# Encoder block on one core: opening stage reordered, factors and copies moved from VectorE to ScalarE

## The chip, the cores and the metric

The kernel runs on one core of one Trainium2 chip. The metric is the device time of one execution in microseconds (us). Engines are named as in the profile: PE (TensorE matmul), PEld (its weight loads), DVE (VectorE), ACT (ScalarE), POOL (GpSimd) and SP (SyncE, which here only issues transfers).

## The reference, cut to what matters

```
mod = silu(c) @ w_ada + b_ada;  shift, scale, gate = split(mod, 3)
h   = rms_norm(x, norm_w) * (1 + scale) + shift          # 1024 x 1024
proj = h @ w_in                                          # eight column groups
r_q, r_k, r_v, r_g, m_cq, m_ckv, m_kr, m_g = split(proj)
rq, rk = rope(r_q, positions), rope(r_k, positions) * 64**-0.5
lg_f, lg_b = log_sigmoid(decay logits)                   # one per head
scores = (q . k) * decay_mask(lg); cross = (q * exp(lg*(i+1))) . state
...                                                      # group norm, attention group, output projection, residual
```

The opening stage computes `h` transposed (the "features"), the first retention projection, and three things that depend on small inputs alone: the decays `lg` with the masks made from them, and the cosine and sine tables of the rotary embedding.

## The kernel before, in words

All matrices are 1024 wide and cut into 128-row tiles: eight feature tiles `k`, eight sequence tiles `t`. Products are made to full precision by splitting each operand into a high and a low part (`hh`/`hl` for features, `wh`/`wl` for weight pages) and adding three matmuls (lines 65 to 67).

The opening goes as follows. `x_tile(t)` squares and sums a tile of x, takes the power on POOL (L158), scales the tile on DVE (L159), transposes it on PE and copies the two halves to `xn`, half 0 by ACT (L166), half 1 by DVE (L168). `modulation(k)` makes two sums over 1024 columns on DVE (L178) and from them two factors per feature (L181, L183). `features(k, half)` applies the factors on ACT (L188), rounds to `hh` on ACT (L189) and takes the rest `hl` on DVE (L190). `products(k, lo, hi)` adds feature tile `k`'s 12 matmuls for four sequence tiles. The eight sums `acc0` occupy all eight PSUM banks until feature 7 is in.

Then each of the four head groups `g` runs: for a tile `t` of sums, ACT copies the value part `v` (L355), DVE multiplies the query and key part by the cosine table `Cr` and the sine table `Sr` (L364, L366), POOL combines (L370, L371), and so on. The first `gate` matmuls of group 0 need a PSUM bank, and that is free only when `v`, L364 and L366 of tile 0 have read it.

A weight page comes through `wpage`: a transfer of 512 KB into one of two `wr` buffers, a cast on ACT (`wh`, L80) and a subtraction (`wl`, L81) on POOL; the four pages of the opening take DVE for that. A third page's transfer must wait for the first page's subtraction.

The program is written as a data flow; a scheduler turns it into one fixed order per engine, and each engine executes its own list in that order. `tc.issue_after(ins)` holds the instructions traced inside it behind `ins` in the list of `ins`'s engine; others of the block are free. Before the change only the masks and the two Sin activations stand behind such a mark (the ACT cast of feature `KACT = 1`); decays (L236 to L260) and table arithmetic (L280 to L315) are placed wherever the scheduler saw room.

Of the kernel before, what the change touches and what calls it, by code (L numbers as in the profile page):

```python
# [12 lines left out]
AF = mybir.ActivationFunctionType  # L13
ALU = mybir.AluOpType
# [16 lines left out]
def body(tc, I, O):  # L31
    nc = tc.nc
    V, A, G, T, SY = nc.vector, nc.scalar, nc.gpsimd, nc.tensor, nc.sync
# [50 lines left out]
    def wpage(src, n, k, pool=None, tag="wr", bufs=2):  # L84
        raw = (pool or p_ring).tile([P, n], F32, name="wr", tag=tag, bufs=bufs)
        SY.dma_start(out=raw, in_=src)
        return split(raw, (("p (k n) -> p k n",), {"k": k}))
# [10 lines left out]
    hh = [p_h.tile([P, S], F32R, name=f"hh{k}", tag=f"hh{k}") for k in range(KT)]  # L98
    hl = [p_h.tile([P, S], F32R, name=f"hl{k}", tag=f"hl{k}") for k in range(KT)]
# [25 lines left out]
    xn = p_st.tile([P, KT, S], F32, name="xn", tag="xn")  # L125
# [22 lines left out]
    def x_tile(t, bank):  # L148

        x_ = ld["x", t]  # L150
        if t in XDVE:
            V.scalar_tensor_tensor(out=xn[:, :, ts_(t)], in0=x_.rearrange("p (a b) -> p a b", b=P), scalar=1.0,
                                   in1=x_.rearrange("p (a b) -> p a b", b=P), op0=ALU.mult, op1=ALU.mult,
                                   accum_out=msq[:, t:t + 1])
        else:
            A.activation(xn[:, :, ts_(t)], x_.rearrange("p (a b) -> p a b", b=P), AF.Square, accum_out=msq[:, t:t + 1])
        V.tensor_scalar(out=msq[:, t:t + 1], in0=msq[:, t:t + 1], scalar1=1.0 / D, scalar2=EPS, op0=ALU.mult, op1=ALU.add)
        G.tensor_tensor(out=r_x[:, t:t + 1], in0=msq[:, t:t + 1], in1=neghalf[:, 0:1], op=ALU.pow)  # L158
        V.tensor_scalar(out=x_, in0=x_, scalar1=r_x[:, t:t + 1], scalar2=None, op0=ALU.mult)  # L159
        for z in range(2):  # L160
            ps = bank()
            for q in range(4):
                T.transpose(ps[:, ts_(q)], x_[:, ts_(4 * z + q)], ident)
            dst, src = xn[:, 4 * z:4 * z + 4, ts_(t)], ps.rearrange("p (a b) -> p a b", a=4)
            if z == 0:
                A.copy(out=dst, in_=src)  # L166
            else:
                V.tensor_copy(out=dst, in_=src)  # L168

    b1s = {}  # L170
    c1 = ctile("c1", KT)
    V.scalar_tensor_tensor(out=c1, in0=bada[:, KT:2 * KT], scalar=1.0, in1=nw, op0=ALU.add, op1=ALU.mult)

    def modulation(k):
        mp = p_st.tile([P, 2], F32, name="mp", tag="mp", bufs=3)
        for i, kind in enumerate("sb"):
            wa = ld[kind, k]
            V.scalar_tensor_tensor(out=wa, in0=wa, scalar=1.0, in1=sc, op0=ALU.mult, op1=ALU.mult,  # L178
                                   accum_out=mp[:, i:i + 1])
        b1 = p_st.tile([P, 2], F32, name="b1", tag="b1", bufs=3)  # L180
        V.scalar_tensor_tensor(out=b1[:, 0:1], in0=mp[:, 0:1], scalar=nw[:, k:k + 1], in1=c1[:, k:k + 1],  # L181
                               op0=ALU.mult, op1=ALU.add)
        V.tensor_tensor(out=b1[:, 1:2], in0=mp[:, 1:2], in1=bada[:, k:k + 1], op=ALU.add)  # L183
        b1s[k] = b1

    def features(k, half):
        sl = slice(half * 512, half * 512 + 512)
        A.activation(xn[:, k, sl], xn[:, k, sl], AF.Identity, bias=b1s[k][:, 1:2], scale=b1s[k][:, 0:1])  # L188
        i0 = A.copy(out=hh[k][:, sl], in_=xn[:, k, sl])  # L189
        V.tensor_tensor(out=hl[k][:, sl], in0=xn[:, k, sl], in1=hh[k][:, sl], op=ALU.subtract)  # L190
        return i0

    w0, acc0 = [], []

# [22 lines left out]
    for k in range(KT):  # L217
        if k:
            modulation(k)
        if k % 2 == 0 and k + 2 < KT:  # L220
            load(("w", k // 2 + 1))
        if 3 <= k + 2 < KT:
            load(("s", k + 2), ("b", k + 2))
        if k and k % 2 == 0:
            w_page(k // 2)
        for half in range(2):
            if k or half:
                i0 = features(k, half)
                products(k, 4 * half, 4 * half + 4)
            if k == KACT:  # L230
                x_last = i0


    lg = ctile("lg", 16)
# [29 lines left out]
    after = ExitStack()  # L264
    after.enter_context(tc.issue_after(x_last.ins))
    for h in range(H):
# [17 lines left out]
                    in1=posf.unsqueeze(2).broadcast_to([P, NT, 32]), op=ALU.mult)  # L284
# [26 lines left out]
    after = tc.issue_after(x_last.ins)  # L311
# [4 lines left out]
    A.activation(Cr, nn, AF.Sin)  # L316
    after.__exit__(None, None, None)

    st.close()


# [14 lines left out]
            pending.pop(0)()  # L336

    for g in range(4):
        w = w0 if g == 0 else [wpage(I["w_ret"][g][j], 1024, 2) for j in range(4)]
        vv = []  # L340
        ST = p_ret.tile([P, NT, 2, P], F32, name="ST", tag="ST")
        sT = [None] * NT
        qdT = [None] * NT
        for t in range(NT):
# [13 lines left out]
            if g == 0 and NACC <= t < NB0:  # L358
# [6 lines left out]
                            in1=Cr[:, t:t + 1].broadcast_to([P, 8, 32]), op=ALU.mult)  # L365
# [23 lines left out]
            for h in range(2):  # L389
# [3 lines left out]
                            op=ALU.mult)  # L393
# [19 lines left out]
                                       op0=ALU.mult, op1=ALU.add)  # L413


        wg = [wpage(I["w_rg"][g][j], 1024, 4) for j in range(2)]
        sg = p_ret.tile([P, 2, S], F32, name="sg", tag="sg")
        def gate(h):
            for half in range(2):
# [494 lines left out]
PREP_0 = (2, 4, 5, 6, 6)  # L914
NB0, NACC, XW = 8, 4, 8
WLX = (6, 7)
XDVE, KACT = (3, 6), 1
MG0 = 2
PEND = 1
EARLY = (2, 6)  # L920
# [70 lines left out]
```

## Time and profile before

| | us |
|---|---|
| median of 3 timed runs (1050.13 to 1053.33) | 1051.39 |
| the profiled execution | 1050.91 |
| its span | 1048.8 |
| PE busy in the span | 1014.0 |
| DVE busy in the span | 565.3 |
| first gate matmul of group 0 starts at | 82.74 |

A span counts from the first to the last instruction; 2.1 us of the execution lie outside it. "Busy" is time in which an engine had an instruction in work. A row of a timeline gives the start, the duration (of all, where x2 or more are merged), the engine, the source line and the operation, then output<-inputs; in brackets the engine's idle time just before and what ended it. Instructions of one engine overlap a little at their ends, so that the next starts some 0.07 us before the end shown.

### The profile page before, as it was taken

The numbers are of one execution on the slowest core, as the hardware profiler recorded it, in microseconds if no ns is written. First come the engines' busy times: TensorE is split into PE (matmuls) and PEld (weight loads), VectorE is DVE, ScalarE is ACT, GpSimd is POOL, SyncE is SP. The second block draws the span as 40 slices with busy tenths as digits, with TensorE's granted clock in tenths as the row PEclk, the third lists the DMA queues.
The fourth block names the chain that finished last, engine by engine and source line by source line (L and its number), as shares of the span: only waits on it lengthen the run. The fifth ranks groups of instructions, "written<-read, shape, count | busy, mean of one in ns | idle before, by whom it ended". The sixth has DMA issues, their size and how long they took to land.

```text
span 1048.8 us, 15165 instructions
## 1 busy us (share of the span) xinstructions
PE 1014.0 (97%) x5704; PEld 885.8 (84%) x5704; DVE 565.3 (54%) x1294; ACT 430.2 (41%) x864; POOL 406.5 (39%) x311
## 2 busy tenths in 40 slices
PE   5899999999999999999999999989999999989998
PEld 4687888888888888998888889879999999878887
DVE  7995447445355433046202116777877787882342
ACT  6654313313312312134322016567777777772100
POOL 2233315313411421125634127943466554873210
PEclk8899999999999999999999999999999999999999
DMA  9721103102101203233744420100000000003522
GB/s 369 263 63 58 41 1 121 41 2 80 61 21 41 66 27 114 82 121 101 236 160 170 157 86 1 41 1 2 21 22 21 2 21 22 21 21 121 172 99 71
DMA packets 30744, 82.27 MB, mean 78 GB/s; under 512 B 3536, under 2 KB 4560, under 8 KB 30672
## 3 DMA queue, kind: packets, MB, share of 16 engines
q1 hardware_dynamic: 25920, 72.92, 20.4%
q10 hardware_dynamic: 4752, 8.39, 2.2%
q8 instruction: 45, 0.74, 0.3%
q14 instruction: 27, 0.22, 0.1%
HBM read 64.52 MB, written 16.78 MB: 78 GB/s over the span
## 4 chain that ended last, share of the span: by engine, by line
PE 48%; DVE 4%; ACT 1%; DMA 1%; issue 1%; POOL 1%; ACTq 0%; DVEq 0%; POOLq 0%
PE pt L763 5%; PE acc L65 4%; PE acc L66 4%; PE sp L65 4%; PE acc L67 4%; PE sp L67 4%; PE sp L66 4%; PE po L66 3%; PE po L67 3%; PE po L65 3%; PE sm L66 1%; PE sm L65 1%; PE sm L67 1%; PE pt L676 1%; PE pt L65 1%; PE pt L67 1%
## 5 line engine op out<-in xcount | busy, mean ns | idle before, releaser
L81 POOL TENSOR_TENSOR wl<-wr,wh 128x1024 fp32r<-128x1024 f32 (+2 forms) x51 | 116.2, 2288 | 172.5 <-ACT wh L80 153.8
L65 PE MATMUL acc<-wh,hh 128*128 128x512 f32 (+2 forms) x352 | 131.1, 372 | 1.7 <-ACT hh L189 1.7
L66 PE MATMUL acc<-wl,hh 128*128 128x512 f32 (+2 forms) x352 | 130.8, 372 | 0.0
L67 PE MATMUL acc<-wh,hl 128*128 128x512 f32 (+2 forms) x352 | 126.6, 368 | 2.1 <-DVE hl L190 2.1
L749 POOL TENSOR_SCALAR pr<-pr,st 128x1024 f32<-128x1024 f32 x62 | 72.1, 1166 | 101.2 <-DVE st L748 77.9
L65 PE MATMUL acc<-hh,wh 128*128 128x512 f32 x256 | 101.1, 395 | 1.8 <-ACT v L355 1.8
L766 DVE TENSOR_TENSOR pl<-pt,ph 128x512 fp32r<-128x512 f32 x128 | 85.7, 683 | 31.2 <-ACT ph L765 31.2
L66 PE MATMUL acc<-hl,wh 128*128 128x512 f32 x256 | 101.0, 394 | 0.0
L67 PE MATMUL acc<-hh,wl 128*128 128x512 f32 x256 | 100.6, 393 | 0.0
L80 ACT CAST wh<-wr 128x1024 fp32r<-128x1024 f32 (+2 forms) x55 | 53.7, 982 | 104.8 <-PE sm L66 45.3
L765 ACT CAST ph<-pt 128x512 fp32r<-128x512 f32 x128 | 73.2, 590 | 27.9 <-PE pt L763 25.8
L747 ACT ACTIVATE pr<-sp,st 128x1024 f32<-128x1024 f32 x62 | 69.5, 1121 | 22.9 <-DVE st L745 22.7
L370 POOL TENSOR_TENSOR rb<-t,t 128x128 f32<-128x128 f32 x32 | 16.1, 502 | 160.4 <-PE sm L379 61.2
L66 PE MATMUL po<-pl,vh 128*128 128x256 f32 x256 | 76.4, 298 | 1.9 <-DVE pl L766 1.9
L744 DVE TENSOR_REDUCE st<-sp 128x1 f32<-128x1024 f32 x62 | 75.4, 1216 | 4.6 <-PE sp L67 4.5
L65 PEld LDWEIGHTS acc<-wh,hh 128*128 128x128 f32 x352 | 67.2, 191 | 10.6 <-ACT hh L189 2.1
L67 PEld LDWEIGHTS acc<-wh,hl 128*128 128x128 f32 x352 | 66.0, 188 | 10.8 <-DVE hl L190 3.0
L66 PEld LDWEIGHTS acc<-wl,hh 128*128 128x128 f32 x352 | 67.3, 191 | 8.6
L65 PE MATMUL po<-ph,vh 128*128 128x256 f32 x256 | 73.7, 288 | 0.0
L763 PE MATMUL pt<-ident,pr 128*128 128x128 f32 x496 | 70.2, 274 | 3.0 <-DVE st L748 2.7
L67 PE MATMUL po<-ph,vl 128*128 128x256 f32 x256 | 72.8, 285 | 0.0
L763 PEld LDWEIGHTS pt<-ident,pr 128*128 128x128 f32 x496 | 58.1, 141 | 7.5 <-issue 2.9
(354 smaller groups left out, 2463.4 us busy)
## 6 DMA issues: line engine op xcount, KB each, us to landing
x<-w_ada SPq DMA_DIRECT2D x16, 512.0 KB, 7.0
wr<-w_ret SPq DMA_DIRECT2D x16, 512.0 KB, 3.5
wr<-w_rg SPq DMA_DIRECT2D x8, 512.0 KB, 3.5
retD<-ro SPq DMA_DIRECT2D x16, 256.0 KB, 2.0
wr<-w_mg SPq DMA_DIRECT2D x8, 512.0 KB, 3.5
wa<-w_ada SPq DMA_DIRECT2D x8, 512.0 KB, 3.7
wr<-w_out SPq DMA_DIRECT2D x8, 512.0 KB, 4.5
wro<-retD SPq DMA_DIRECT2D x8, 512.0 KB, 3.9
```

The costliest lines, as they stand in the source:

```text
L65: T.matmul(out, lh, rh, start=first, stop=False, **kw)
L66: T.matmul(out, lh, rl, start=False, stop=False, **kw)
L67: return T.matmul(out, ll, rh, start=False, stop=last, **kw)
L80: A.copy(out=hi, in_=raw)
L81: eng.tensor_tensor(out=lo, in0=raw, in1=hi, op=ALU.subtract)
L370: G.tensor_tensor(out=rv[:, :, 0], in0=t1[:, :, 0], in1=t2[:, :, 1], op=ALU.subtract)
L744: V.tensor_reduce(out=st_[:, 0:1], in_=sp, op=ALU.max, axis=AX.X)
L747: A.activation(pr, sp, AF.Exp, bias=st_[:, 1:2], scale=sc_, accum_out=st_[:, 2:3])
L749: G.tensor_scalar(out=pr, in0=pr, scalar1=st_[:, 3:4], scalar2=0.0, op0=ALU.mult, op1=ALU.add)
L763: T.transpose(tp[:, ts_(q)], pr[:, ts_(half * 4 + q)], ident)
L765: A.copy(out=ph[half][:, :, c_], in_=tv)
L766: V.tensor_tensor(out=pl[half][:, :, c_], in0=tv, in1=ph[half][:, :, c_], op=ALU.subtract)
```

## The change

Four parts. (1) The copies of half 1 of tiles 0 to 3 go from DVE to ACT, and so does the square of tile 3 (`XDVE`). (2) The two factors per feature tile are made by ACT activations on [128 x 1] operands and no longer by DVE. (3) Every DVE instruction of the decays, masks and tables stands behind the `hl` subtraction of feature 5 (`KACT = 5`, `late`), and their marked ACT instructions behind its cast. (4) The ACT casts of the next weight pages (two gate pages of group 0, four pages of group 1) stand behind the last feature cast `f_last`. The transfers are on SP's list and carry no mark; the POOL subtractions follow their casts.

```
-            if z == 0:
+            if z == 0 or t < 4:
                 A.copy(out=dst, in_=src)
...
-        V.scalar_tensor_tensor(out=b1[:, 0:1], in0=mp[:, 0:1], scalar=nw[:, k:k + 1], in1=c1[:, k:k + 1],
-                               op0=ALU.mult, op1=ALU.add)
-        V.tensor_tensor(out=b1[:, 1:2], in0=mp[:, 1:2], in1=bada[:, k:k + 1], op=ALU.add)
+        A.activation(b1[:, 0:1], mp[:, 0:1], AF.Identity, bias=c1[:, k:k + 1], scale=nw[:, k:k + 1])
+        A.activation(b1[:, 1:2], mp[:, 1:2], AF.Identity, bias=bada[:, k:k + 1])
...
             if k == KACT:
-                x_last = i0
+                x_last, v_last = i0
+
+    f_last = i0[0]
+    late = ExitStack()
+    late.enter_context(tc.issue_after(v_last.ins))
...
+    late.close()
     st.close()
...
     for g in range(4):
+        after = ExitStack()
+        if g < 2:
+            after.enter_context(tc.issue_after(f_last.ins))
         w = w0 if g == 0 else [wpage(I["w_ret"][g][j], 1024, 2) for j in range(4)]
+        after.close()
...
+        after = ExitStack()
+        if g == 0:
+            after.enter_context(tc.issue_after(f_last.ins))
         wg = [wpage(I["w_rg"][g][j], 1024, 4) for j in range(2)]
+        after.close()
...
-XDVE, KACT = (3, 6), 1
+XDVE, KACT = (6,), 5
```

What became of the order shows at the hand-over from the last feature to the first gate matmul. ACT's list before, from the last feature casts (`hh_91`) to the copies of `v`:

```order
L189 CAST hh_91<-xn 128x512 x2
L272 ACTIVATE mask<-mt 128x128 x2
L80 CAST wh<-wr 128x1024
L313 ACT_TABLE_LOAD
L313 ACTIVATE Sr<-rtmp 128x256
L316 ACTIVATE Cr<-rtmp 128x256
L80 CAST wh<-wr 128x1024
L355 COPY v<-acc 128x256 x4
```

The same stretch of ACT's list in the changed program, from the instruction behind the last `hh_91` on (line numbers there are shifted by -1 to +12; left out are the three small decay activations L261, L262 and L259):

```order
L80 CAST wh<-wr 128x1024 x4
L316 ACT_TABLE_LOAD
L316 ACTIVATE Sr<-rtmp 128x256
L319 ACTIVATE Cr<-rtmp 128x256
L261 ACT_TABLE_LOAD
...
L270 ACTIVATE qfac<-small,lgs 128x128 x8
L275 ACTIVATE mask<-mt 128x128
L80 CAST wh<-wr 128x1024
L275 ACTIVATE mask<-mt 128x128 x2
L80 CAST wh<-wr 128x1024
L275 ACTIVATE mask<-mt 128x128 x5
L363 COPY v<-acc 128x256 x4
```

Between the last feature cast and the first copy of `v` there are now six page casts, two table loads, and all of `qfac` and `mask`; a third table load, for the decays' first Exp, stands just ahead of the last `hh_91`.

DVE's list before, ahead of the first product with `Cr` (L364), where the masks were long made:

```order
L291 SCALAR_TENSOR_TENSOR rtmp<-rtmp 128x256 x2
L310 TENSOR_SCALAR rtmp<-rtmp 128x256
L314 SCALAR_TENSOR_TENSOR rtmp<-rtmp 128x256
L315 TENSOR_SCALAR rtmp<-rtmp 128x256
L364 TENSOR_TENSOR t_759<-acc,Cr 128x256
L366 TENSOR_TENSOR t_760<-acc,Sr 128x256
```

and in the changed program (`rtmp` is the tables' scratch, `m_` and `mt` the masks' exponents; L372 and L374 are the old L364 and L366):

```order
L318 TENSOR_SCALAR rtmp<-rtmp 128x256
...
L252 SCALAR_TENSOR_TENSOR lg<-lt_628,lt_629 128x16
...
L273 TENSOR_SCALAR m_669<-small,lg 128x128
L274 SCALAR_TENSOR_TENSOR mt<-small,lg,m_669 128x128
...
L273 TENSOR_SCALAR m_711<-small,lg 128x128
L274 SCALAR_TENSOR_TENSOR mt<-small,lg,m_711 128x128
L277 TENSOR_SCALAR mask<-mask 128x1024
L372 TENSOR_TENSOR t_759<-acc,Cr 128x256
L374 TENSOR_TENSOR t_760<-acc,Sr 128x256
```

Eight pairs of mask exponents and the scaling of the whole mask, which waits for the last mask activation, now stand between the end of the tables and the first product with `Cr`.

## Rows read from the trace of the kernel before

**Rows 1.** Busy time by stretch; columns: length, five engines, PE clock, DMA share, GB/s

```profile
0.00:10.00 10.00, 4.72 (x21) 4.46 (x22) 4.38 (x28) 7.15 (x12) 1.83 (x8) 1.00 0.81 301
10.00:20.00 10.00, 5.51 (x29) 4.72 (x27) 9.64 (x27) 5.41 (x10) 2.56 (x3) 0.84 1.03 413
60.00:250.00 190.00, 187.57 (x986) 158.94 (x985) 106.54 (x303) 59.20 (x146) 58.74 (x61) 1.00 0.14 45
```

**Rows 2.** Timeline of PE: products of the opening, then the first gate matmul

```profile
34.01 0.80 PE L65 MATMUL sm<-wh,hh 128*128 128x512 f32 x1 [2.60 <-ACT hh L189]
...
51.13 0.63 PE L65 MATMUL acc<-wh,hh 128*128 128x512 f32 x1
51.56 0.63 PE L66 MATMUL acc<-wl,hh 128*128 128x512 f32 x1
...
80.29 0.39 PE L66 MATMUL sm<-wl,hh 128*128 128x512 f32 x1
80.52 0.39 PE L67 MATMUL sm<-wh,hl 128*128 128x512 f32 x1
82.74 0.47 PE L65 MATMUL acc<-hh,wh 128*128 128x512 f32 x1 [1.84 <-ACT v L355]
```

**Rows 3.** Timeline of POOL: subtractions of weight pages

```profile
46.25 5.92 POOL L81 TENSOR_TENSOR wl<-wr,wh 128x1024 fp32r<-128x1024 f32 x2 [18.61 <-ACT wh L80]
62.57 5.84 POOL L81 TENSOR_TENSOR wl<-wr,wh 128x1024 fp32r<-128x1024 f32 x2 [10.40 <-DVE mt L271]
...
74.39 2.64 POOL L81 TENSOR_TENSOR wl<-wr,wh 128x1024 fp32r<-128x1024 f32 x1
```

**Rows 4.** Timeline of DVE: instructions that ran beside those, and L364

```profile
47.02 2.31 DVE L181 SCALAR_TENSOR_TENSOR b<-mp,small,c 128x1 f32<-128x1 f32 x1
...
49.85 3.40 DVE L178 SCALAR_TENSOR_TENSOR x<-x,sc 128x1024 f32<-128x1024 f32 x1
...
74.71 2.60 DVE L291 SCALAR_TENSOR_TENSOR rtmp<-rtmp 128x256 f32<-128x256 f32 x1
...
81.84 0.42 DVE L364 TENSOR_TENSOR t<-acc,Cr 128x256 f32<-128x256 f32 x1 [1.83 <-ACT v L355]
```

**Rows 5.** Timeline of DVE: the same kinds of instruction undisturbed

```profile
22.66 0.34 DVE L271 SCALAR_TENSOR_TENSOR mt<-small,lg,m 128x128 f32<-128x128 f32 x1
...
27.78 0.74 DVE L159 TENSOR_SCALAR xl<-xl,r_x 128x1024 f32<-128x1024 f32 x1
28.45 1.21 DVE L178 SCALAR_TENSOR_TENSOR x<-x,sc 128x1024 f32<-128x1024 f32 x1
...
29.59 0.68 DVE L168 COPY xn<-sm 128x512 f32<-128x512 f32 x1
30.19 0.20 DVE L181 SCALAR_TENSOR_TENSOR b<-mp,small,c 128x1 f32<-128x1 f32 x1
...
38.30 0.68 DVE L190 TENSOR_TENSOR hl<-xn,hh 128x512 fp32r<-128x512 f32 x1
...
73.88 0.91 DVE L274 TENSOR_SCALAR mask<-mask 128x1024 f32<-128x1024 f32 x1
...
78.00 0.88 DVE L291 SCALAR_TENSOR_TENSOR rtmp<-rtmp 128x256 f32<-128x256 f32 x2
```

**Rows 6.** Timeline of ACT

```profile
38.26 1.85 ACT L267 ACTIVATE qfac<-small,lgs 128x128 f32<-128x128 f32 x6
...
61.45 1.04 ACT L80 CAST wh<-wr 128x1024 fp32r<-128x1024 f32 x1
...
64.59 1.52 ACT L188 ACTIVATE xn<-xn,b 128x512 f32<-128x512 f32 x2
...
69.81 1.12 ACT L189 CAST hh<-xn 128x512 fp32r<-128x512 f32 x2
...
74.33 1.28 ACT L313 ACT_TABLE_LOAD   x1
```

**Rows 7.** Transfers issued in the first 100 us: KB each, median us to landing

```profile
wr<-w_ret SPq DMA_DIRECT2D x9, 512.0 KB, 3.5
```

More of the change, by code (lines that the diff above doesn't have):

```diff
@@ L189, in features @@
         i0 = A.copy(out=hh[k][:, sl], in_=xn[:, k, sl])
-        V.tensor_tensor(out=hl[k][:, sl], in0=xn[:, k, sl], in1=hh[k][:, sl], op=ALU.subtract)
-        return i0
+        i1 = V.tensor_tensor(out=hl[k][:, sl], in0=xn[:, k, sl], in1=hh[k][:, sl], op=ALU.subtract)
+        return i0, i1
     w0, acc0 = [], []
```

## Prediction

> **What bounds the kernel now.** I read the busy time by stretch first. After 60 us PE is the bound and hardly waits: busy 187.57 of 190 us in the stretch to 250 [rows 1]. So whatever moves the start of that stretch moves the end of the kernel by the same amount, and the question is when PE can start its first gate matmul, at 82.74 in the profiled execution [rows 2].
>
> Next I read PE's own timeline. Its last product of the opening starts at 80.52, then it waits 1.84 us for ACT's copy of v and for what stands behind that, because all eight PSUM banks hold sums that nobody has read [rows 2]. The hand-over (tables ready, v copied, L364 and L366 done, PE starts) is the place that sets everything behind it. Before it PE is fed by DVE: in 10 to 20 us DVE is busy 9.64 of 10 us, PE 5.51 [rows 1].
>
> Third, POOL and DVE side by side. Two page subtractions on POOL run from 46.25 to 52.17 and one from 74.39 to 77.03 [rows 3]. Beside the first two, a DVE instruction on 128x1 elements takes 2.31 us and one on 128x1024 takes 3.40; beside the third, L291 takes 2.60 [rows 4]. Undisturbed the same kinds take 0.20, 1.21 and 0.46 (half of 0.88, with the step to the next) [rows 5]. So each subtraction stops DVE for 2.1 to 2.2 us. The two subtractions at 62.57 do it twice more: five of five that met such DVE work. One DVE instruction gets through between two subtractions that follow each other.
>
> **What the change gives the opening.** DVE loses four copies (0.60 each, from one start to the next), one square (1.14) and 16 factors (about 0.13 each): 5.6 us. It also loses the decays, masks and tables ahead of feature 5, and the two stops of 2.2 us at 46 to 52, since those casts now stand behind the last feature. ACT gains 4 copies, a square and 16 small activations, and has room.
>
> How early the last feature cast, T, then comes, by DVE's list: the first w_ada row cannot be in before 0.29 + 5 x 0.524 = 2.9 MB have arrived, 9.7 us at 301 GB/s; the second needs about 11 us [rows 1]. From there to the last of the 16 sums DVE has 16 x 1.14 (L178) + 5 x 0.67 (L159) + 5 x 1.14 (four page subtractions and the square of tile 6) + 4 x 0.60 (L168) + 10 x 0.60 (L190) + 0.4 of small ones = 36.1 us [rows 5]. I add 2.5 us for waits on ACT's first page cast and on POOL's powers (an estimate; 0 to 5), which gives 49.6. Then ACT: factors 0.2, two L188 1.4, a cast 0.5, the table load 1.28, an Exp 0.1, the last cast 0.5 [rows 6]: T = 53.7, where the features before ran to about 71.
>
> PE does not reap it there. Its 180 products behind 34.01 cost 0.227 us each, 41 us [rows 2]; started 2 to 4 us earlier and without stalls they end at 72 to 75 instead of 81. Then the banks are full, as before.
>
> **What the change puts on the hand-over.** Behind T, ACT's list has four page casts, Sin, Exp, qfac, masks with two more casts, and only then the copies of v. Counted from T:
>
> First the tables. The casts (0.95 each) let POOL subtract from T+1.0 to T+6.9 (2.9 each, as in the disturbed pairs [rows 3]). The third page's transfer waits for the first subtraction and lands 3.5 us after its issue [rows 7], so it is cast at T+8.4 and subtracted until T+11.1; the fourth is cast at T+11.4 and subtracted until T+14.1. DVE has 18 table instructions behind the last hl: 11 at 0.46 and 7 single-source ones at about 0.3, 7.2 us [rows 5]. Between the stops it gets 0.95, 0.6, 2.1 and 0.6 us; the other 2.9 follow T+14.0. The last one that Sr needs ends at T+16.9, Cr is complete at **T+18.1**.
>
> Then the masks, counted from Cr: an Exp load 1.28, three small Exp 0.5, eight qfac 2.35 (6 took 1.85), a mask 0.2, the fifth page's cast 0.95 [rows 6]. So the fifth and sixth subtractions run from +5.3 to +11.1 and stop DVE in the middle of the mask exponents, of which only two are buffered. The rest, a remainder of 0.3 and three pairs at 0.6, ends at +13.0; the last mask activation 0.25, the scaling of the mask 0.83 (L274), and two products with Cr and Sr 0.75: PE starts at **Cr + 14.9** [rows 4, 5].
>
> Sum: 53.7 + 18.1 + 14.9 = 86.7 against 82.74, **+4.0 us**. PE has then been idle for 12 to 14 us. In the opening, after 2.60 us of idleness, and again near 51, products start 0.43 us apart instead of 0.227, the lower of the clock's two levels (1.2 GHz) [rows 2]; that lasted for 8 and about 10 products, 1.6 and 1.9 us lost. I take +1.7 (0, as after the 1.84 us of idleness, to 3.5). Together +5.7 on the execution of 1050.91: **1056.6 us**. That execution is 0.5 below the median of the three timed runs, 1051.39, so this is +0.5% on the median.
>
> The remaining edits cost nothing of their own. The factors' ACT activations lie under DVE's sums, which ACT waits for anyway; if ACT had no room there, 32 halves of features would shift by some 0.1 us each, before T. Page transfers for group 1 are issued by SP in the same sequence, and its pages are needed only after four gate passes of 24 products, 20 us behind the hand-over.
>
> Two rules of the Trainium skill bear on this. The page "SBUF — State Buffer", section "SBUF: two separate sides", says that VectorE and GpSimd share one port pair as an exclusive lock, that a VectorE instruction with two SBUF inputs or in a two-port mode needs it, and that the loser blocks for the whole instruction. The rows show 2.1 to 2.2 of 2.6 to 2.9 us; by the rule the six stops would be some 0.3 us longer each, and the sum about 1.5 us more, 1058. "ScalarE: Activation LUTs", section "What ACT_TABLE_LOAD costs", puts a drain of about 1.38 us on top of 1.28 for each switch. The row shows 1.28; by the rule the two loads on the path (ahead of T, and behind Cr) would add 2.8 us, 1059.4.
>
> **The rivals.** (a) *The stops do not add up: faster.* If POOL's subtractions find gaps of DVE's chain, whose instructions wait for one another, or delay only work that ACT's list delays anyway, the tables are bound by the casts: two subtractions of 2.4 end at T+5.8, the fourth cast at T+10.3, Sin load, Sr and Cr at T+12.4, and the masks take 10.0 instead of 14.9. PE starts at 53.7 + 22.4 = 76.1, waits 1 to 4 us, loses 1.6 to the clock: 77.7, -5.0, 1046 us. Were the tables ready before PE, the floor is PE's own 72 to 75: 1042. Against it: five of five stops. The six stops cost the path 10.6 us in the sum (5.7 in the tables, 4.9 in the masks); the sign turns where they cost less than 4.9, and the gain can be told below 1.7.
>
> (b) *Only the tables are stopped.* The fifth and sixth casts come where DVE has the mask exponents done, or POOL gets the lock late: 53.7 + 18.1 + 10.0 = 81.8, +1.7 clock: +0.8, 1051.7, no difference that can be told. For it: the mask exponents are short, so a race of 0.3 us decides one of them.
>
> (c) *Worse:* DVE waits more in the opening (T at 57), or the later pages land 2 us later each with transfers under way: +3 to +4 on the sum, 1060.5.
>
> (d) *The opening is not relieved at all,* because transfers bound it: 28 tiles of 0.524 MB at 413 GB/s end near 38 us, ahead of the last sums at 48. T moves only if this were 10 us off; I leave it in (c).
>
> **How the numbers follow.** The sum as made: 0.57; (c) and (d): 0.06; (b): 0.15; (a): 0.22. Faster by over 0.3% (3.2 us, about what a measurement of this kernel can tell from no change) is (a), 0.22. Within it: (b) and a small part of the sum with T at 51, together 0.17. Slower 0.61. The sum's own range is 1053.5 to 1060.5 (T 2.5 us either way, the clock 0 to 3.5). The range for 8 in 10 has to reach into (a), down to 1046, where half of (a) lies, and up to 1061.5 for most of (c).
>
> **What the profile after would show.** Right, step by step: the last feature cast at 52 to 56; no DVE instruction of the features above 2 us; PE's products unbroken from some 31 us and done at 72 to 75; four subtractions on POOL within 14 us behind the last cast, each with one DVE table instruction of about 2.5 us beside it; Cr some 18 us behind the last cast; two more such pairs among the mask exponents; an idle time of PE of 10 us and more that ends with L374 or the copy of v; products 0.43 apart after it. Wrong: an idle time of PE under 5 us there, tables' instructions at 0.4 beside the subtractions, or a last feature cast before 50.

## The result: 0.6% slower

The changed kernel takes 1056.16 us (median of 6 runs, 1054.07 to 1056.76); the kernel before, run beside it, 1050.14 (6 runs, 1047.92 to 1053.33). The ratio is 1.0056, 95% interval 1.0039 to 1.0073. Forecast were 1056.6 us and slower with a chance of 0.61. The profiled execution took 1055.9 us with a span of 1053.8, so 5.0 more than the profiled one of before; by the medians the changed kernel takes 6.0 more.

I read the changed kernel's profile in the order of the prediction: busy time by stretch first, columns as in [rows 1].

```profile
10.00:20.00 10.00, 4.49 (x26) 3.67 (x27) 6.47 (x12) 8.88 (x18) 2.56 (x3) 0.71 1.03 412
20.00:30.00 10.00, 8.55 (x44) 7.17 (x42) 9.19 (x17) 6.40 (x14) 4.39 (x3) 0.78 1.03 409
...
80.00:90.00 10.00, 0.74 (x2) 0.67 (x3) 8.85 (x14) 4.41 (x15) 5.31 (x6) 0.50 0.30 105
...
60.00:250.00 190.00, 174.96 (x916) 148.13 (x914) 103.07 (x304) 57.83 (x148) 57.47 (x58) 0.96 0.15 51
```

From 60 to 250 us TensorE is now busy 174.96 us instead of 187.57 [rows 1]. The loss lies at the hand-over: in the row from 80 to 90 us TensorE is busy 0.74 us, at a granted clock of 0.50. In the two stretches of the opening VectorE has 3.5 and 0.8 us to spare; in the first of them it had 0.4 before. This comes up again below. TensorE's own timeline has the place itself (start, duration, operation, and the idle time with what ended it):

```profile
73.83 0.39 PE L67 MATMUL sm<-wh,hl 128*128 128x512 f32 x1
89.26 0.76 PE L65 MATMUL acc<-hh,wh 128*128 128x512 f32 x1 [15.04 <-DVE t L374]
89.83 0.63 PE L66 MATMUL acc<-hl,wh 128*128 128x512 f32 x1
90.25 0.63 PE L67 MATMUL acc<-hh,wl 128*128 128x512 f32 x1
```

The opening's products are done at 74.2 instead of 80.9 [rows 2], and nothing comes of it: TensorE idles 15.04 us, starts its first gate product 6.5 us later than before, and then has starts 0.42 to 0.43 us apart, the lower level of the clock. What it waited for stands on GpSimd and VectorE. First GpSimd's timeline of the changed kernel from 55 to 92 us:

```profile
57.22 4.94 POOL L81 TENSOR_TENSOR wl<-wr,wh 128x1024 fp32r<-128x1024 f32 x2 [30.64 <-ACT wh L80]
64.27 5.17 POOL L81 TENSOR_TENSOR wl<-wr,wh 128x1024 fp32r<-128x1024 f32 x2 [2.11 <-DVE lt L249]
79.32 4.69 POOL L81 TENSOR_TENSOR wl<-wr,wh 128x1024 fp32r<-128x1024 f32 x2 [9.88 <-ACT wh L80]
```

Beside these, in VectorE's timeline of the same stretch, stand six instructions over 2 us:

```profile
57.34 2.37 DVE L244 TENSOR_TENSOR lt<-lt,lt 128x16 f32<-128x16 f32 x1
...
59.83 2.36 DVE L245 TENSOR_TENSOR lt<-lt 128x16 f32<-128x16 f32 x1
...
64.49 2.37 DVE L248 TENSOR_TENSOR lt<-lt,lt 128x16 f32<-128x16 f32 x1
...
67.12 2.36 DVE L249 TENSOR_SCALAR lt<-lt 128x16 f32<-128x16 f32 x1
...
79.49 2.33 DVE L274 SCALAR_TENSOR_TENSOR mt<-small,lg,m 128x128 f32<-128x128 f32 x1 [0.47 <-ACT mask L275]
81.85 2.74 DVE L273 TENSOR_SCALAR m<-small,lg 128x128 f32<-128x128 f32 x1
```

Six page subtractions, six instructions of VectorE that take 2.33 to 2.74 us instead of the 0.17 to 0.35 that the same kinds take elsewhere in this timeline; these are the lines that answer to [rows 3, 4]. ScalarE's timeline of the changed kernel, in the same stretch, shows the chain that runs through them:

```profile
54.16 1.28 ACT L241 ACT_TABLE_LOAD   x1
...
55.58 0.61 ACT L188 CAST hh<-xn 128x512 fp32r<-128x512 f32 x1
56.10 1.99 ACT L80 CAST wh<-wr 128x1024 fp32r<-128x1024 f32 x2
...
73.45 0.42 ACT L319 ACTIVATE Cr<-rtmp 128x256 f32<-128x256 f32 x1 [0.37 <-DVE rtmp L318]
73.89 1.28 ACT L261 ACT_TABLE_LOAD   x1
75.18 0.30 ACT L261 ACTIVATE kfac<-lg,small 128x8 f32<-128x8 f32 x1
...
87.64 1.18 ACT L363 COPY v<-acc 128x256 f32<-128x256 f32 x4
```

The last feature cast ends at 56.2 (the expectations below say 56.1, which is where the next cast starts), Cr is complete at 73.87, and the copies of v start only at 87.64, behind the last mask.

### The profile page after: what moved, and what is told of

It is laid out like the page before. It is cut to its first block, busy times and chain, and to the rows that moved or that the text cites. A ratio compares the mean times of both kernels' runs of the same rounds, so it can differ in the third digit from the quotient of the medians.

```text
span 1053.8 us, 15175 instructions
## 1 busy us (share of the span) xinstructions
PE 1011.0 (96%) x5704; PEld 884.5 (84%) x5704; DVE 559.5 (53%) x1272; ACT 439.2 (42%) x887; POOL 404.7 (38%) x311
## 4 chain that ended last, share of the span: by engine, by line
PE 48%; DVE 3%; ACT 1%; DMA 1%; issue 1%; POOL 1%; ACTq 0%; DVEq 0%; POOLq 0%
PE pt L775 5%; PE acc L65 4%; PE sp L65 4%; PE acc L66 4%; PE acc L67 4%; PE sp L67 4%; PE sp L66 4%; PE po L66 3%; PE po L67 3%; PE po L65 3%; PE sm L66 1%; PE sm L65 1%; PE sm L67 1%; PE pt L688 1%; PE pt L65 1%; PE pt L66 1%
## 5 line engine op out<-in xcount | busy, mean ns | idle before, releaser
L80 ACT CAST wh<-wr 128x1024 fp32r<-128x1024 f32 (+2 forms) x55 | 53.7, 982 | 112.4 <-PE sm L66 42.3
L65 PEld LDWEIGHTS acc<-hh,wh 128*128 128x128 f32 x256 | 48.5, 189 | 25.3 <-ACT v L363 15.4
```

Source lines behind the costliest of these rows:

```text
L65: T.matmul(out, lh, rh, start=first, stop=False, **kw)
L80: A.copy(out=hi, in_=raw)
```

## The experiments

The theory that went into them: each GpSimd subtraction that runs beside tables or masks holds one VectorE instruction for its whole length, these stops add up along the chain from the last feature to the v copies, and TensorE, with all banks full, waits for that chain. The main rival (A): the order on ScalarE (casts, table loads, qfac, masks, then v) sets the hand-over, whatever GpSimd does.

**1. The stops taken away.** The edit, on the changed kernel as in all runs (here and below a long line is cut to the call that changes, and lines that only hand an argument on are left out):

```diff
+        if not low:
+            A.copy(out=hi, in_=raw)
+            v_ = hi.rearrange(*shape[0], **shape[1])
+            return v_, v_
...
-wpage(I["w_ret"][g][j], 1024, 2)
+wpage(I["w_ret"][g][j], 1024, 2, low=g != 1)
-wpage(I["w_rg"][g][j], 1024, 4)
+wpage(I["w_rg"][g][j], 1024, 4, low=g > 1)
```

> The changed kernel, with the low halves of the weight pages behind the features (w_ret of the second group, w_rg of the first two) left out: their high half stands in for it, so GpSimd has no subtraction between the features and the masks. Loads, casts, table loads and the order on ScalarE stay. My theory (six GpSimd subtractions each stop one table or mask instruction of VectorE for 2.1 to 2.5 us, and the chain from Cr to the v copies hands that on): the stopped instructions go back to 0.2 to 0.4 us, Cr complete 7 to 9 us sooner (65 to 67 instead of 73.9), the first gate product at 76 to 79 instead of 89.3, TensorE's wait before it 2 to 5 us instead of 15.0, time 1042 to 1046. Rival A (ScalarE's list decides: three table loads, four casts, eight qfac, eight masks ahead of the v copies, whatever GpSimd does): gate product at 86 or later, time 1053 to 1057. Rival B (only the stops in the tables lie on the path, those in the masks are hidden): gate product at 80 to 82, 1047 to 1050.

Measured: 1052.88 us, ratio to before 1.0022 (1.0012 to 1.0033). GpSimd has no subtraction between the features and the gate product, the tables' instructions take 0.16 to 0.43 us each and the masks' exponents 0.28 to 0.35. This kernel's timeline of TensorE has the end of the opening and the first gate product:

```profile
74.31 0.39 PE L67 MATMUL sm<-wh,hl 128*128 128x512 f32 x1
79.30 0.77 PE L65 MATMUL acc<-hh,wh 128*128 128x512 f32 x1 [4.59 <-DVE t L378]
```

The gate product comes at 79.30, 10.0 us sooner than with the stops, after 4.59 us of idleness instead of 15.04. That was the theory's number (76 to 79) within 0.3 us, and rival A's (86 or later) is off by 7. 0.9 of the 10.0 us is an earlier last feature cast (55.3). Cr is complete at 67.6, not quite at the expected 65 to 67. ScalarE's timeline of this kernel has the reason:

```profile
64.51 1.05 ACT L80 CAST wh<-wr 128x1024 fp32r<-128x1024 f32 x1 [1.21 <-DMA wr<-w_ret]
...
67.20 0.40 ACT L323 ACTIVATE Cr<-rtmp 128x256 f32<-128x256 f32 x1
```

With no subtraction to wait for, a fifth page is cast ahead of the table load, and Sr and Cr follow that load without a wait: once the stops are gone, the page casts and the transfers that they wait for set Cr. In all, seven page casts stand ahead of v here instead of six, so ScalarE has more to do there than in the changed kernel, and rival A is out all the same. Rival B (gate product at 80 to 82) is only 0.7 us off; against it stands that the gate product follows Cr by 11.7 us here and by 15.4 in the changed kernel. The total is not what I expected: 3.3 us below the changed kernel instead of 10 to 14. The lead is 9.1 us at TensorE's matmul 400, counted from 0 (106.88 against 115.96), and 8.1 at matmul 3600 (712.26 against 720.34), but 4.3 at matmul 4200 (800.25 against 804.53). It goes in the attention stage, far from the edited pages; from 720 to 780 us TensorE is busy 58.98 us there, where the changed kernel has 60.00. The next part comes back to that.

**2. The tables early again, all else kept.**

```diff
-    late.enter_context(tc.issue_after(v_last.ins))
...
-XDVE, KACT = (6,), 5
+XDVE, KACT = (6,), 1
```

> The changed kernel without its part that puts decays, masks and rotary tables behind the features; copies and factors on ScalarE stay, and so do the pages held behind the last feature. My theory (the table and mask work between features and v copies, with the stops in it, makes the hand-over late; taken into the features it fills VectorE there at its undisturbed price): last feature cast 4 to 8 us later than 56.1 (60 to 64), but Cr and the masks ready within 12 to 16 us of it, first gate product at 76 to 80, time 1043 to 1049, so faster than both. Rival (the held pages are the cost, wherever the tables stand): gate product at 86 or later, time 1053 to 1057. Rival C (VectorE's sum is what counts and nothing is gained by order): gate product at 82 to 84, time 1049 to 1052.

Measured: 1044.76 us, ratio 0.9954 (0.9938 to 0.9971): faster than before, and 11.4 us below the changed kernel. This kernel's timeline of ScalarE, with the last feature casts and the first copies of v:

```profile
54.61 1.12 ACT L188 CAST hh<-xn 128x512 fp32r<-128x512 f32 x2
...
76.79 1.19 ACT L362 COPY v<-acc 128x256 f32<-128x256 f32 x4
```

And of TensorE, its one wait from 70 to 95 us:

```profile
78.09 0.47 PE L65 MATMUL acc<-hh,wh 128*128 128x512 f32 x1 [1.59 <-ACT v L362]
```

The time and the gate product are as expected, one number is not: I had the last feature cast at 60 to 64, since VectorE now does decays, masks and part of the tables ahead of it. It ends at 55.7, as early as with the late tables (56.2). From 10 to 30 us VectorE is busy 18.4 us here against 15.7 in the changed kernel (busy time by stretch of experiment 2; columns: length, VectorE's busy time, TensorE's clock, DMA share, GB/s):

```profile
10.00:20.00 10.00, 8.87 (x27) 0.82 1.03 413
20.00:30.00 10.00, 9.56 (x17) 0.84 1.03 409
```

The early decays and masks fill time in which VectorE otherwise waits (for what, the groups under experiment 7 show). With the pages held, as here, taking them out gave the features nothing; putting them behind the features added them to the chain.

**3. The pages no longer held.**

```diff
-        if g < 2:
-            after.enter_context(tc.issue_after(f_last.ins))
...
-        if g == 0:
-            after.enter_context(tc.issue_after(f_last.ins))
```

> The changed kernel without the hold of the next weight pages behind the last feature; copies, factors and the late tables stay. My theory (the pages find a free buffer and a place on ScalarE only near the end of the features anyway, so their subtractions meet the tables with or without the hold): first two subtractions at 54 to 58, still four stops of 2.1 to 2.4 us in the tables, gate product at 86 to 90, time 1053 to 1057, same as the changed kernel within 0.3%. Rival (the hold is what moved the subtractions onto the tables): subtractions beside the features, at most two stops in tables and masks, gate product at 78 to 82, time 1045 to 1050.

Measured: 1057.65 us, ratio 1.0070 (1.0055 to 1.0085). First subtractions at 56.58, four table instructions and two of the masks beside them, gate product at 88.46. This is as expected, save that the time is 0.65 us over the range. Once the tables are late, the hold by itself brings the last feature cast from 58.0 to 56.2 and does nothing for the gate product (89.26 with it), since the pages' casts stand in nearly the same place without it (the first pair at 55.46, just ahead of the last feature cast). TensorE's one wait in this kernel's timeline from 70 to 95 us:

```profile
88.46 0.77 PE L65 MATMUL acc<-hh,wh 128*128 128x512 f32 x1 [13.40 <-DVE t L372]
```

**4. Copies and factors on ScalarE alone** (the edits of experiments 2 and 3 together, which leave the kernel before with the first two parts of the change).

> The kernel before with only the copies of four tiles and the modulation factors on ScalarE: tables, decays and masks early, pages not held. My theory (these two parts alone relieve VectorE by some 5 to 7 us in the features and add no stops): last feature cast at 62 to 66, gate product at 77 to 81, time 1044 to 1050, faster than before. Rival (TensorE or ScalarE bounds the opening once VectorE is relieved, or page subtractions then stop the features): gate product at 81 to 83, time 1049 to 1052, no change from before.

Measured: 1048.37 us, ratio 0.9977 (0.9968 to 0.9987). Last feature cast at 62.5, gate product at 79.27, both in the theory's range. Two pairs of subtractions still run beside the features (from 50.21 and from 61.50 on) and stop instructions of tables and masks there. Against experiment 2 this also prices the hold where the tables are early: it brings the last feature cast from 62.5 to 55.7, the gate product by 1.2 us, the time by 3.6 us (2.2 in the profiled executions); what the time gains beyond the gate product is not explained.

**5. The four w_ret pages held behind the masks instead of behind the features**.

```diff
+        m_last = A.activation(mask[:, h], mt, AF.Exp)
...
-            after.enter_context(tc.issue_after(f_last.ins))
+            after.enter_context(tc.issue_after((f_last, m_last)[g].ins))
```

> The changed kernel, all work kept, with the four w_ret pages of the second group held behind the last mask exponent instead of the last feature; the two w_rg pages stay where they are. My theory (each GpSimd subtraction in the tables or masks costs its stop): the first pair still stops two table instructions (about 2.2 us each above their 0.17), the other four stops are gone, Cr complete about 4.4 us sooner (69 to 70), two more page casts stand ahead of the v copies (up to 2.0 us), first gate product at 80 to 83, time 1047 to 1051. Rival A (ScalarE's list decides): gate product at 86 or later, 1053 to 1057. Rival B (the stops only move into the rotation of the first tiles, and the next pages come late to TensorE): gate product at 80 to 83, but TensorE then waits 4 us or more for wl of the second group before 130 us, time 1052 to 1056.

Measured: 1049.82 us, ratio 0.9992 (0.9983 to 1.0001). Two stops are left ahead of the gate product, and each quantity falls as the theory had it: Cr at 69.6, gate product at 81.78, time inside 1047 to 1051; the next pages are not late. VectorE's instructions over 2 us in this kernel, from 54 to 92 us:

```profile
57.00 2.36 DVE L244 TENSOR_TENSOR lt<-lt,lt 128x16 f32<-128x16 f32 x1
...
59.48 2.37 DVE L245 TENSOR_TENSOR lt<-lt 128x16 f32<-128x16 f32 x1
...
86.94 2.32 DVE L380 COPY rb<-rb 128x192 f32<-128x192 f32 x1
...
89.19 2.62 DVE L382 TENSOR_TENSOR kd<-rb,kfac 128x256 f32<-128x256 f32 x1
```

Its timeline of ScalarE has Cr and the first copies of v:

```profile
69.20 0.42 ACT L319 ACTIVATE Cr<-rtmp 128x256 f32<-128x256 f32 x1 [0.37 <-DVE rtmp L318]
...
80.48 1.19 ACT L363 COPY v<-acc 128x256 f32<-128x256 f32 x4
```

This run confirms the first with all the work done: two stops less in the tables, Cr 4.25 us earlier. (The third and the fourth, at 86.94 and 89.19, hit the work on the first tiles, behind the gate product.)

**6. Early tables, and the w_ret pages behind Cr as well.** The edits of 2 and, with `cr_last = A.activation(Cr, nn, AF.Sin)`, the hold of 5 on `cr_last`.

> The version with early tables (1044.8), with the four w_ret pages of the second group held behind Cr as well. My theory: there the first gate product came 1.6 us after TensorE had run out of opening products, so at most 1.6 us are to be had from the two stops that are left in the tables; gate product at 76 to 77.5, the wait of TensorE under 1 us, time 1042 to 1045, no change from that version within 0.3%. Rival (stops in the tables still cost 2.2 us each): time 1040 to 1041. Rival (pages late to TensorE): 1046 or more.

Measured: 1044.60 us, ratio 0.9941 (0.9923 to 0.9958), no difference from experiment 2 that can be told. TensorE has no wait at all at the hand-over now; the first gate product is at 76.97. Busy time by stretch of this kernel, columns as in [rows 1]:

```profile
70.00:80.00 10.00, 10.00 (x46) 8.29 (x45) 4.27 (x11) 5.56 (x13) 7.34 (x7) 1.00 0.28 105
```

With this the hand-over is bound by TensorE's own products; nothing more is to be had there.

**7. Late tables and held pages without the copies and factors.**

```diff
-            if z == 0 or t < 4:
+            if z == 0:
...
-        A.activation(b1[:, 0:1], mp[:, 0:1], AF.Identity, bias=c1[:, k:k + 1], scale=nw[:, k:k + 1])
-        A.activation(b1[:, 1:2], mp[:, 1:2], AF.Identity, bias=bada[:, k:k + 1])
+        V.scalar_tensor_tensor(out=b1[:, 0:1], in0=mp[:, 0:1], scalar=nw[:, k:k + 1], in1=c1[:, k:k + 1],
+                               op0=ALU.mult, op1=ALU.add)
+        V.tensor_tensor(out=b1[:, 1:2], in0=mp[:, 1:2], in1=bada[:, k:k + 1], op=ALU.add)
...
-XDVE, KACT = (6,), 5
+XDVE, KACT = (3, 6), 5
```

> The changed kernel without its two first parts: copies of four tiles, square of the fourth tile and modulation factors back on VectorE; late tables and held pages stay. My theory (the late chain from the last feature cast to the gate product is a fixed 33 us, with its six stops, and the copies and factors set when it begins): last feature cast 4 to 8 us later than 56.1 (60 to 64), gate product at 93 to 97, time 1060 to 1064. Rival (TensorE's products or ScalarE set the opening, VectorE's relief does nothing): gate product at 88 to 91, time 1055 to 1058.

Measured: 1057.66 us, ratio 1.0068 (1.0050 to 1.0086): my numbers were wrong and the rival's right, though its reason (the relief does nothing) is not what the trace shows. The last feature cast ends at 58.2, 2.1 us later than in the changed kernel, not 4 to 8, and the gate product comes at 89.04, no later at all. The groups of VectorE's instructions from 8 to 57 us tell why, this kernel's first (busy us and mean ns of one, then the idle time before them and what ended it):

```profile
L159 DVE TENSOR_SCALAR x<-x,r_x 128x1024 f32<-128x1024 f32 x5 | 3.8, 750 | 1.3 <-POOL r_x L158 1.3
...
L168 DVE COPY xn<-acc 128x512 f32<-128x512 f32 x4 | 2.7, 684 | 0.0
L181 DVE SCALAR_TENSOR_TENSOR b<-mp,small,c 128x1 f32<-128x1 f32 x8 | 1.7, 216 | 0.0
...
L183 DVE TENSOR_TENSOR b<-mp,small 128x1 f32<-128x1 f32 x8 | 1.2, 155 | 0.0
...
L152 DVE SCALAR_TENSOR_TENSOR xn<-x 128x1024 f32<-128x1024 f32 x1 | 1.2, 1215 | 0.0
```

The same groups view of the changed kernel, with the instructions that wait:

```profile
L159 DVE TENSOR_SCALAR x<-x,r_x 128x1024 f32<-128x1024 f32 x6 | 4.5, 753 | 3.5 <-POOL r_x L158 3.5
...
L159 DVE TENSOR_SCALAR xl<-xl,r_x 128x1024 f32<-128x1024 f32 x2 | 1.5, 748 | 0.4 <-POOL r_x L158 0.4
...
L157 DVE TENSOR_SCALAR msq<-msq 128x1 f32<-128x1 f32 x7 | 1.1, 151 | 1.6 <-ACT xn L156 1.5
```

The work put back is 2.7 + 1.7 + 1.2 + 1.2 = 6.8 us. In the changed kernel VectorE has waited 3.5 + 0.4 us for GpSimd's r_x and 1.6 for squares on ScalarE, 5.5 us; here 1.3 + 0.7 (the 0.7 again for squares). So about half of the relief turned into waiting. And only three stops stood ahead of Cr (at 59.41, 61.96 and 66.53); the fourth page was cast behind the Sin load and stopped L251 at 73.03, behind Cr. So Cr came 15.0 us after the last feature cast, not 17.7, and the later start was made up.

**8. The six subtractions on VectorE.**

```diff
-wpage(I["w_ret"][g][j], 1024, 2)
+wpage(I["w_ret"][g][j], 1024, 2, eng=V if g == 1 else G)
-wpage(I["w_rg"][g][j], 1024, 4)
+wpage(I["w_rg"][g][j], 1024, 4, eng=V if g == 0 else G)
```

> The changed kernel, all work kept, with the six page subtractions behind the features on VectorE instead of GpSimd (there such a 128x1024 subtraction takes 1.22 us in the opening's four pages). My theory (a GpSimd subtraction costs VectorE its whole length less one small instruction, 2.1 to 2.5 us; so VectorE does it itself more cheaply): VectorE's chain loses 13.3 us of stops and gains 7.3 us of subtractions, the gate product comes 3 to 7 us sooner than 89.3 (82 to 86), time 1048 to 1053. Rival A (ScalarE's list decides): 86 or later, 1053 to 1057. Rival B (the stop is hidden time, the subtraction on VectorE is added time): 90 or later, 1057 or more.

Measured: 1053.44 us, ratio 1.0033 (1.0022 to 1.0044); gate product at 86.02, 3.2 us sooner than in the changed kernel. That is the theory's slow end for the gate product, 0.4 over its time; both numbers lie in rival A's ranges too, so this run does not tell the two apart, as experiments 1 and 5 do. No stop is left ahead of Cr, but five page subtractions of 1.22 us stand there on VectorE, and Cr comes 16.4 us after the last feature cast instead of 17.7. A later page's subtraction was moved up into the masks on GpSimd and made one stop again (78.60, 2.32 us), which the theory had not counted.

**9. The six subtractions cut into four GpSimd instructions each** (parts=4 for these pages).

```diff
-        eng.tensor_tensor(out=lo, in0=raw, in1=hi, op=ALU.subtract)
+        for i in range(parts):
+            s_ = slice(i * n // parts, (i + 1) * n // parts)
+            eng.tensor_tensor(out=lo[:, s_], in0=raw[:, s_], in1=hi[:, s_], op=ALU.subtract)
```

> The changed kernel, all work kept, with each of the six page subtractions behind the features cut into four GpSimd instructions of 128x256. My theory (a stopped VectorE instruction waits for the end of the one GpSimd instruction that is running, and one VectorE instruction passes before the next): 24 GpSimd instructions of 0.6 to 0.7 us, stops of 0.5 to 0.6 us instead of 2.1 to 2.4, four times as many table instructions pass beside the subtractions, gate product 1 to 5 us sooner (84 to 88), time 1050 to 1055. Rival (a stop has a fixed price of some 2 us, or one goes with each GpSimd instruction): twice as many stops or more at 2 us, gate product at 95 or later, time over 1060. Rival B (VectorE waits until GpSimd's queue of ready work is empty): no instruction passes between the quarters, gate product at 89 to 91, time 1056 to 1058.

Measured: 1051.41 us, ratio 1.0011 (1.0001 to 1.0020); gate product at 85.40. This kernel's timeline of GpSimd, with the quarters:

```profile
57.46 7.17 POOL L83 TENSOR_TENSOR wl<-wr,wh 128x256 fp32r<-128x256 f32 x8 [31.25 <-ACT wh L80]
65.50 3.63 POOL L83 TENSOR_TENSOR wl<-wr,wh 128x256 fp32r<-128x256 f32 x4 [0.86 <-DVE rtmp L296]
71.75 2.87 POOL L83 TENSOR_TENSOR wl<-wr,wh 128x256 fp32r<-128x256 f32 x4 [2.62 <-ACT wh L80]
77.65 5.72 POOL L83 TENSOR_TENSOR wl<-wr,wh 128x256 fp32r<-128x256 f32 x8 [3.03 <-DVE mt L276]
```

And of VectorE beside the first eight of them:

```profile
57.58 0.71 DVE L246 TENSOR_TENSOR lt<-lt,lt 128x16 f32<-128x16 f32 x1
...
58.41 0.70 DVE L247 TENSOR_TENSOR lt<-lt 128x16 f32<-128x16 f32 x1
...
59.24 0.71 DVE L250 TENSOR_TENSOR lt<-lt,lt 128x16 f32<-128x16 f32 x1
```

The stop shrinks with the GpSimd instruction: the same 128x16 operations take 0.70 us instead of 2.36. So an instruction of VectorE waits for the end of the one GpSimd instruction that runs, and in the tables mostly one more gets in before the next. Rival B (nothing passes until GpSimd has no more work ready) is out. Of the first rival one half is right: each of the 24 quarters stops one instruction, but at 0.3 to 0.6 us and not at 2. Per page the tables gain nothing by that, since four stops of 0.53 us are 2.1. Cr comes 15.6 us after the last feature cast instead of 17.7 because fewer stops stand ahead of it (6.4 us instead of 8.8): the fourth page is cast behind the Sin load, as in experiment 7, and its quarters (from 71.75) run behind Cr, where VectorE waits for ScalarE's first mask anyway. The masks do gain: their last eight quarters hold VectorE 2.8 us above the undisturbed times, where the two whole subtractions cost 4.4.

All together, in us of the profiled executions (last feature cast, Cr complete, first gate product) and the median time:

| kernel | feature cast | Cr | gate product | time |
|---|---|---|---|---|
| before | 70.9 | 80.5 | 82.74 | 1050.1 to 1050.8 |
| changed | 56.2 | 73.9 | 89.26 | 1056.16 |
| 1 no low halves | 55.3 | 67.6 | 79.30 | 1052.88 |
| 2 tables early | 55.7 | 74.6 | 78.09 | 1044.76 |
| 3 pages free | 58.0 | 73.6 | 88.46 | 1057.65 |
| 4 copies and factors only | 62.5 | 77.0 | 79.27 | 1048.37 |
| 5 w_ret pages behind masks | 55.8 | 69.6 | 81.78 | 1049.82 |
| 6 tables early, pages behind Cr | 56.4 | 71.1 | 76.97 | 1044.60 |
| 7 late, without copies | 58.2 | 73.2 | 89.04 | 1057.66 |
| 8 subtractions on VectorE | 55.5 | 71.9 | 86.02 | 1053.44 |
| 9 subtractions in quarters | 56.4 | 72.0 | 85.40 | 1051.41 |

The features are the same in the changed kernel and in experiments 1, 5, 8 and 9, and their last cast lies between 55.3 and 56.4: a difference of 1 us between two single profiles says little.

## Why the prediction was right, step by step

**The bound and the place.** Right in the main. What moves the first gate product moves the end, but only to within a few us: in experiment 1 the gate product came 3.4 us sooner than in the kernel before and the end 2.4 later (see the sum below). The opening's products ended at 74.2 (72 to 75 foreseen), unreaped, banks full.

**T, the last feature cast: 56.2 instead of 53.7.** The 52 to 56 given as a sign of being right is missed by 0.2. The first sum started at 11.3 (11 foreseen), the last ended at 51.7, not 49.6; ScalarE's part behind them was 4.4 instead of 4.1 (its terms as listed give 4.0). VectorE between the first sum and the last, in the changed kernel (length, VectorE's busy time, TensorE's clock, DMA share, GB/s):

```profile
11.34:51.75 40.41, 36.73 (x64) 0.83 0.80 308
```

Its work was 36.7 us where 36.1 were foreseen, and its waits were 3.7 us. The sum had "2.5 us for waits on ACT's first page cast and on POOL's powers", 0 to 5; so the term was 1.2 too small, inside its range. Of the 3.7 us, 1.9 were waits for powers and 0.2 for the page cast; the other 1.5 were for a square on ScalarE, which the term did not name. (The 5.5 us under experiment 7 count from 8 us on.)

The step's reasoning also failed in one point that the number hides. It counts decays, masks and tables as time that VectorE gets back ahead of T. Experiment 2 shows that with the pages held they gave T nothing (55.7 with them early). The copies and factors brought T from 70.9 to 62.5 (experiment 4). From there either of the other two edits brings it down, and they do not add up: the hold to 55.7 (experiment 2), which takes page casts and subtractions out of the features (experiment 4 has the first pair from 50.21 on), the late tables to 58.0 (experiment 3), both to 56.2. In experiment 3 the first page casts moved too, from 49.08 to 55.46, so what the late tables alone do for T without the hold is not shown.

**The tables: Cr at T + 17.7 instead of T + 18.1.** Right, with the subtractions about where they were foreseen (57.22 and 64.27, T + 1.0 and T + 8.1, for T + 1.0 and T + 8.4) and 2.2 us above the undisturbed time for each stop. The 7.2 us of VectorE's own work were right by luck: the trace has 20 table instructions at 0.34 or 0.21 us from start to start, 5.7 us, and between them the decays, which the step left out; their 15 small instructions that were not stopped took 1.7 us.

**The masks: Cr + 15.4 instead of + 14.9.** Right, although the terms as listed give + 15.0 (11.1, 0.3 and three pairs at 0.6 are 13.2 and not 13.0). The fifth and sixth subtractions came at Cr + 5.45 (foreseen + 5.3) and each stopped a mask exponent. Rival (b), in which these are hidden, is out by this and by experiment 1: there the gate product follows Cr by 11.7 us, so the two stops cost 3.7 (foreseen 4.9). The load at 73.89 takes 1.28 us and the next activation starts at 75.18, right behind it. The 1059.4 by the rule of "ScalarE: Activation LUTs" (the Trainium skill), section "What ACT_TABLE_LOAD costs", was too long: no drain comes on top of a load here.

**The price of the stops.** Foreseen: 10.6 us of the path. Experiment 1 takes them away: Cr comes at T + 12.3 instead of T + 17.7, and the gate product 11.7 us behind Cr instead of 15.4. So the stops cost 5.4 and 3.7, 9.1 us together (foreseen 5.7 and 4.9). Rival (a) needed them to cost under 4.9. It was right in one thing: without the stops the tables are bound by the casts, and Cr comes close to its T + 12.4, though behind five casts and not four. So the path lost 5.4 us to the tables' four stops, which held VectorE for 8.8. A stopped instruction ends with the subtraction: the first of the pair at 57.22 takes 2.46 us and the 2.37 us of L244 from 57.34 on end 0.03 later. The rule in the Trainium skill's page "SBUF — State Buffer", section "SBUF: two separate sides", by which the loser of the port pair is blocked for the whole instruction of the other engine, agrees in kind with experiment 9: 2.36 us beside a whole page, 0.70 beside a quarter. The 1058 us by that rule needed stops some 0.3 us longer than 2.2; the six held VectorE for 13.2 us in all, 2.2 each.

**The clock.** Foreseen 1.7 us. From 89.26 on one step of 0.57 us and seven of 0.42 to 0.43, instead of 0.227, are 1.7 us.

**The sum.** Hand-over +6.5 instead of +4.0, nearly all of the difference T's 2.5 us; with the clock +8.1 at TensorE's matmul 400 (115.96 against 107.84), where +5.7 was foreseen. The end is +5.0 in the profiled executions. So that the forecast came out closer than its terms is luck: T was 2.5 too early, and 3 us came back later. By matmul 2600 the distance is 7.0 (517.64 against 510.60), at 3400 still 7.1 (686.30 against 679.24), at 3600 5.7 (720.34 against 714.64), at the last 5.1. In the step from 3400 to 3600 TensorE waits 2.6 us in the kernel before and 1.8 in the changed one. The view of TensorE's waits from 680 to 720 us, of the kernel before (total, times, longest):

```profile
PE pt L763 <- DVE st L745: 2.6, 1, 2.6
```

And of the changed one:

```profile
PE sp L65 <- ACT epr L718: 1.8, 1, 1.8
```

The two programs don't have the same order of instructions there, nor do all of the experiments: the scheduler that orders each engine's list answers an edit in the opening with small changes in the attention stage too (on TensorE between matmuls 3500 and 4022). The kept traces hold that order fixed in groups while the opening changes: from 200 us on experiments 5, 7 and 9 have the order of the kernel before on TensorE, VectorE, ScalarE and GpSimd, experiment 8 has that of the changed kernel, and experiments 2, 4 and 6 share a third, from which experiment 3 departs in a few instructions of ScalarE and VectorE. The time from matmul 3400 to matmul 4200:

| order | kernel or experiment | us |
|---|---|---|
| of the changed kernel | changed, 8 | 118.2, 118.3 |
| of the kernel before | 5, 7, 9 | 118.5, 118.4, 118.4 |
| of the kernel before | before | 119.6 |
| third | 2, 4, 6 | 119.9, 120.0, 119.8 |
| nearly the third | 3 | 120.4 |
| experiment 1's own | 1 | 122.7 |

Within an order the time hardly depends on the opening, so the 4.5 us that experiment 1 loses here against the changed kernel go with its order, though no other run has that order. What the changed kernel gets back is another matter. The kernel before takes 119.6 us with an order that took three other openings 118.4 to 118.5, and experiment 7, with that order and its gate product at 89.04, gets back 1.1 of the changed kernel's 1.3 us. So the order gives little of it. The rest of the 3 us lies ahead of matmul 2600 (1.1) and behind 4200 (0.6). Its cause stays open; single executions of the kernel before differ by more than that (1047.92 to 1053.33).

## What to carry to other kernels

Small VectorE work that fills the waits of a stage can be free there (experiment 2); put alone between two stages it costs its full price, and a stop for each GpSimd instruction that runs beside it, so look at what a moved step stood beside and at what will run beside it then. With all buffers full, earlier inputs bring nothing: follow the chain to whatever frees a buffer (here decays, tables, masks, the copies of v). Undo the parts of a change one by one: here copies, factors and held pages are worth 0.5% (1044.8 us), and the late tables cost 1.1% (1044.8 to 1056.2), which the sum of them hid.

## What the hardware showed that I had not expected

An instruction of VectorE on 128x16 elements (0.17 us) is held by a GpSimd subtraction of 128x1024 as long as a larger one: 2.36 to 2.37 us in the four cases in the tables. And cutting the GpSimd instruction in four paid here although GpSimd gets slower by it: its 24 pieces of experiment 9 take 7.17 + 3.63 + 2.87 + 5.72 = 19.4 us (0.72 to 0.91 each on the mean of a group), where the six whole ones took 4.94 + 5.17 + 4.69 = 14.8; the gate product still came 3.9 us sooner, for the two reasons given there: the fourth page behind Cr, and shorter stops among the masks.
